# A hybrid encoder block on one core: where the rows of the stream's blocks begin, and how query and key columns are cut

## The chip, the core and the metric

The kernel runs on one core of one Trainium2 chip. The time is device time in microseconds (us) of one execution, and of several runs the median is given. The profile is one execution taken by the hardware profiler. Engines are named as the profile does: PE is TensorE's matmul side, PEld its weight loads, DVE is VectorE, ACT is ScalarE, POOL is GpSimd, SP is SyncE, whose queue issues most transfers.

## The reference

One layer of a streaming encoder over 1040 positions (16 meta tokens and 1024 frames) of width 1024, float32:

```
h = concatenate([meta, x])
h = h + token_mixer(rmsnorm(h), w_in, ..., w_out)      # 4 mLSTM heads and 4 retention heads
h = h + channel_mixer(rmsnorm(h), w_up, w_gate, ffn_conv_w, w_down)
return rmsnorm(h)[16:]

channel_mixer(u): a = causal_dwconv(u @ w_up, 3 taps)
                  (silu(a) * (u @ w_gate)) @ w_down    # width 2816
```

The mixer projects to queries, keys, values and gates, runs a short convolution or a rotation on queries and keys, scans both kinds of heads in chunks, normalises each head, gates it and projects back with w_out.

## The kernel before

**Precision.** Each large product is made of three float32r matmuls: an operand x is kept as hi (rounded) and lo (x minus hi), and hi*hi, hi*lo and lo*hi are added in one PSUM bank. `mm3s` issues the three; its lines are L924 (hi weights, hi stream), L925 (hi weights, lo stream) and L926 (lo weights, hi stream). The first operand is stationary (a 128x128 weight tile), the second moves, up to 512 columns at a time.

**Seven products for eight.** The large products are cut into 2x2 quarters and computed with seven products of sums and differences. So the stream is kept not as two halves but as blocks, one for each of the seven operands. In the gated MLP the blocks are numbered 0 to 6, each a hi and a lo tile of four rows (one for each 128 of the contraction), and each row holds XW = 514 columns: two columns of halo that the 3-tap convolution needs, and 512 of the stream. `ublock` and `fblock` make them: blocks 0, 3, 4 and 5 in the u-tiles (PE rows name them uh_g and ul_g), block 1 in two large tiles (x), blocks 2 and 6 in the pool `fp` (xh and xl). Before, the four rows of a block follow each other at a distance of 514 columns, 2056 bytes.

**The stages in time.** Up to some 673 us: normalisation, the projections of one head after another (`qk_steps`, `o_steps`, `v_steps`), and between their matmuls the side work of the heads (scans, convolutions, normalisations). This side work is dealt into the stream of matmuls by a planner: `watch` keeps a modelled time for each engine (a float32r matmul of n columns counts 0.004 + 0.000445 n us, at least 0.107), and `slot` and `tick` compare these loads with limits (`RULES`) to decide how much side work follows each step. The order that they deal is pinned for PE, DVE and ACT. Query and key products go through `qk_steps`, which cuts the 528 columns of a half at FMC; `v7_steps` uses the same cut. Output gates are cut at OC = [(14, 272), (272, 528)].

From 673 to some 855 us: the output projection (`mixw`, an object of the class `Seven`; PSUM tiles pwx and pwy). Its moving operands alternate between the tiles `fraw` (rows wr) and two ring tiles `rring` (rows rr), as `wr` picks them; one of its five steps has its weights split early into four tiles (w4xh, w4xl) that `four` makes.

From some 845 to 1296 us: the gated MLP's up and gate products. The first pair of column blocks runs over `eight` (`first_up`, `first_gate`); the ten others run over `seven`: seven products, each of four rows times three matmuls, for the gate with one chunk of 512 columns (2 to 514 of a row), for up with the two chunks of UC. Weights are loaded, summed and split by `fstep`, which uses a scratch tile s1.

From 1296 us on: the down projection (`down`, class `Seven`; PSUM tiles pdx and pdy), whose moving operands are slots of the u-tiles, and for the second half of its last quarter 22 small tiles r4h and r4l; then the final normalisation and the output.

**Memory.** Pools on the left grow from the low end of each of the 128 partitions, pools with side="right" from the high end downwards: first `mxp`, later `accp` (the ring tiles), `fp2`, `fp4`, `d2` and `d3` (the r4 tiles). The tiles of the ring begin 32 bytes past a multiple of 64, and so do the r4 tiles, w4xh and block tiles xh.

The one line of `seven` that reads a block, j0 and j1 being the chunk's columns:

```
m = mm3s(pt, [tuple(v[:, o*HB + k*P : o*HB + (k+1)*P] for v in (hi, lo)) for k in range(4)],
         [tuple(v[:, k, j0:j1] for v in xs) for k in range(4)], fresh, n in (1, 5, 6))
```

Of the kernel before, what the change touches and what calls it, by code (L numbers as in the profile page):

```python
# [10 lines left out]
F32 = mybir.dt.float32  # L11
F32R = mybir.dt.float32r
# [5 lines left out]
P = 128  # L18
# [3 lines left out]
SEQ = 1024  # L22
T = META + SEQ
# [6 lines left out]
KD = NFB // 2  # L30
HB = 4 * P
XW = SEQ // 2 + 2
EPS = 1e-6
NEG = -1e30
KSCALE = 128.0 ** -0.5
UN = 1024
SB = 528
# [52 lines left out]
def body(ctx, tc, h_in, vecs, cst, mask_in, rot, w_v0, w_vp, w_g, w_out, w_up, w_gate, w_down, out):  # L90
# [18 lines left out]
    G, PE, V, AC = nc.gpsimd, nc.tensor, nc.vector, nc.scalar  # L109
# [97 lines left out]
    upool = Slots(tc, ctx.enter_context(tc.tile_pool(name="upool", bufs=1)), 1)  # L207
    mix = ExitStack()
    st = Slots(tc, mix.enter_context(tc.tile_pool(name="st", bufs=1)), 1)
    wk = Slots(tc, mix.enter_context(tc.tile_pool(name="wk", bufs=2)), 2)  # L210
    mixed = ExitStack()
    mxp = Slots(tc, mixed.enter_context(tc.tile_pool(name="mxp", bufs=1, side="right")), 1)
    accseg = ExitStack()

    def big(tag, nm, dt=F32R):
        return upool.tile([P, 4 * SB], dt, tag=tag, name=nm)

    def blk(x):
        return x.rearrange("p (k j) -> p k j", k=4)
# [52 lines left out]
    xload(0)  # L272
    V.memset(epsc, EPS)
    V.tensor_scalar(vec[:R36, V_N + 1:V_N + 2], vec[:R36, V_BI:V_BI + 1], 1.0 / 15.0, None, ALU.mult)
# [11 lines left out]
    def pp(name, tag):  # L286
        return ps.tile([P, 512], F32, tag=tag, name=name, bufs=PSB[tag])
# [183 lines left out]
    done = Ready()  # L471
# [316 lines left out]
    def fstep(u, s):  # L788
        kind, i = fseq[u]
        nm = f"{kind}{i}_{s}"  # L790
        fetch(u)
        (w11, w12, r0), (w21, w22, r1) = fraws[u]
        if s:
            fetch(u + 1)
        if u < 2:
            return fsplit(nm, [(r0, r1)[s]])
        if s == 0:
            return fsplit(nm, [r0])
        if s == 1:
            s1 = fpool[0].tile([P, HB], F32, tag="s1", name=f"s1_{u}", bufs=1)  # L800
            V.tensor_tensor(s1, w21, w22, ALU.add)
            V.tensor_tensor(w21, w21, w11, ALU.subtract)
            V.tensor_tensor(w11, s1, w11, ALU.subtract)
            return fsplit(nm, [w11, s1])
        if s == 2:
            V.tensor_tensor(w12, w12, w11, ALU.subtract)
            return fsplit(nm, [w21, w12])
        return fsplit(nm, [w22])
# [231 lines left out]
                steps.append(step)  # L1040
        return steps

    FMC = [(0, 264), (264, SB)]
    OC = [(KEEP, 272), (272, SB)]
    QUAD = {0: (0, 0), 1: (0, 0), 2: (1, 0), 5: (1, 0), 3: (1, 1), 4: (1, 1), 6: (0, 1)}

# [288 lines left out]
    QT = HALF // 2  # L1335
# [159 lines left out]
    wslots = {}  # L1495
# [14 lines left out]
    fpool = []  # L1510
# [26 lines left out]
    def four(x, i):  # L1537
        if ("four", x, i) not in wslots:
            tag = f"x{x}{(2, 6)[i]}"
            wslots["four", x, i] = fpool[0].tile([P, 4 * XW], F32R, name="w4" + tag, tag=tag, bufs=1)  # L1540
        return wslots["four", x, i]

    def wbank(nm, b, j):
# [98 lines left out]
    def post_steps(h, p):  # L1642
# [4 lines left out]
        def stats():  # L1647
            num, mv, den = outs.pop(p)
            z = mxp.tile([P, 4], F32, tag="z", name=f"z{h}_{p}", bufs=4)
            if h < H:  # L1650
# [3 lines left out]
                V.tensor_tensor(z[:, :n], z[:, :n], e2, ALU.max)  # L1654
                V.scalar_tensor_tensor(z[:, :n], z[:, :n], EPS, mv[:, 0:n, 1], ALU.mult, ALU.add)
                yield
# [53 lines left out]
    side = []  # L1710
# [122 lines left out]
    s1 = [st.tile([P, 2 * SB], F32, tag=f"A{i + 1}", name=f"s1_{i}").rearrange("p (k j) -> p k j", k=2) for i in range(2)]  # L1833
# [117 lines left out]
    for k in range(KW):  # L1951
        if k % 2 == 0:
            x = upool.tile([P, 2 * T], F32R, tag=("uh0", "ul0", "uh1", "ul1")[k // 2], name=f"wone{k}")
# [31 lines left out]

    TA, TB = KEEP, KEEP + XW - 2
    blocks = {}

    def xb(i):
        return blocks[i]  # L1990
# [15 lines left out]
    def ftile(nm):  # L2006
        return fp.tile([P, XW + 2], F32, tag="f", name=nm, bufs=5)

# [6 lines left out]
    def spare_out(nm):  # L2015
        return fp4.tile([P, XW + 2], F32, tag="xc", name=nm, bufs=2)

# [45 lines left out]
    def scale_tasks(t0, t1, tag):  # L2063
# [4 lines left out]
        def one(kb):  # L2068
            x = RES[kb][:, t0:t1]
            V.tensor_tensor(x, x, Rb[:, t0:t1], ALU.mult)  # L2070
            last["scaled"] = xsingle(kb, t0, TA + XW if t1 == TB else t1, t0 >= TB)
        return [norm] + [lambda kb=kb: one(kb) for kb in range(KB)]
# [14 lines left out]
    fp = fseg.enter_context(tc.tile_pool(name="fp", bufs=2, reuse_waits="tile"))  # L2087
    Rb = fp.tile([P, T], F32, name="Rb", tag="Rb", bufs=1)
# [15 lines left out]
        wload("A2", k)  # L2104

    def ublock(i):
        return tuple(upool.tile([P, 2 * T], F32R, tag=f"u{x}{i}", name=f"u{x}{i}_g")[:, :4 * XW].rearrange("p (k j) -> p k j", k=4) for x in "hl")

    def fblock(b):
        if b == 5:  # L2110
            return tuple(big(f"t{i}", f"x{i}5")[:, :4 * XW].rearrange("p (k j) -> p k j", k=4) for i in range(2))
        return tuple(fp.tile([P, 4, XW], F32R, name=f"x{x}{b}", tag=f"x{x}{b}", bufs=1) for x in "hl")


    BQ, AQ = [(MB, T)], [(MA, MA + QT), (MA + QT, MB)]
    side = []
# [5 lines left out]
    for t, (st, k) in enumerate(mixw.steps):  # L2122
        if st == "2":
            break
        if t < KW - 2:
            continue
        if st == "65" and k == 5:
            x = fp.tile([P, 4 * XW], F32, name="wm", tag="xl6", bufs=1)
            nc.sync.dma_start(x[:, :2 * D].rearrange("p (k j) -> p k j", k=2), w_out[14:16].rearrange("k p j -> p k j"))
        if st == "65" and k >= 2:  # L2130
            after(mixw.tsum(3, k - 2), last["rsplit"][1])
        elif st == "73" and k < 2:
            after(mixw.tsum(3, KW - 2 + k), last["rsplit"][1])
        if t >= KW - 2:
            mixw.prep(t)
            if t < KW:
                mixw.mms(t)
        for u in range(t, min(t + (3 if st == "4" or t == KW - 2 or (st, k) == ("73", KW - 1) else 2), 4 * KW)):
            mixw.prep(u)
            if mixw.steps[u][0] == "73" and u % 2 and u + 7 not in mixw.four:  # L2140
                mixw.pre4(u + 7)
        if t >= KW:
            mixw.mms(t)
        if st == "4" and k == 0:
            for _ in tail_sum(7, [x[:, b * D:(b + 1) * D] for b in range(2)]):
                pass
        if st == "4" and k == 1:
            pe = pp("pe2", "tr")
            for j in range(2):
                PE.transpose(pe[:, j * P:(j + 1) * P], tail[:, j * P:(j + 1) * P], ident)  # L2150
            for i, y in enumerate(RT):
                V.tensor_tensor(y[:, :, T - 2:], y[:, :, T - 2:], pe[:, :2 * P].rearrange("p (j g t) -> p j g t", j=2, g=4)[:, :, i, :2], ALU.add)
        if st == "4" and k:
            some(3)
        if k == KW - 1:
            mixw.give(st)
            if st == "73":
                for b in (2, 6):
                    blocks[b] = fblock(b)
                side += norm_tasks(*BQ[0]) + scale_tasks(*BQ[0], "tr")  # L2160
# [84 lines left out]
    c0 = {}  # L2245
    gbank = {}
    kept = {(kind, m, half): dram.tile([P, n], F32, name=f"kept_{kind}{m}{half}") for kind, n in (("up", XW), ("ga", HB)) for m in range(2) for half in range(2)}
    UC = [(0, QT), (QT, XW)]

    def eight(kind, half, j0, j1, bank, done):  # L2250
        for m in range(2):
            hi, lo = need((kind, 0, m), 2 - m)
            pt = bank(m)[:, :j1 - j0]
            xs = [xb(kb // 4 if half == 0 else (6, 2)[kb // 4]) for kb in range(KB)]
            mm3s(pt, [tuple(y[:, kb * P:(kb + 1) * P] for y in (hi, lo)) for kb in range(KB)],
                 [tuple(y[:, kb % 4, j0:j1] for y in xs[kb]) for kb in range(KB)], True, True)
            done(m, pt)

    def first_up(half, ci, tags):
        def done(m, pt):  # L2260
            if ci == 0:
                c0[m, half] = ftile(f"c0_{m}{half}")
            AC.copy(c0[m, half][:, slice(*UC[ci])], pt)
            if ci:
                nc.sync.dma_start(kept["up", m, half], c0[m, half][:, :XW])
        eight("up", half, *UC[ci], lambda m: pp(f"pup0_{m}{half}{ci}", tags[m]), done)

    def first_gate(half, j0, j1, tags):
        def bank(m):
# [33 lines left out]
        xcomb(k, QT, XW)  # L2303

    def up_part(i):
        chunks = UC
        def done(m, half, c):
            if isinstance(c, list):
                t = ftile(f"c{i}_{m}{half}")
                for x, (j0, j1) in zip(c, chunks):  # L2310
                    AC.copy(t[:, j0:j1], x)
                c = t
            conv(i, m, half, c)
        return seven("up", i, chunks, done)
# [54 lines left out]
    for i in range(1, NPAIR):  # L2369
        u, g = up_part(i), gate_part(i)  # L2370
# [30 lines left out]
    Rb = dp.tile([P, T], F32, name="Rc", bufs=1)  # L2401
# [78 lines left out]
    for p in (1, 2):  # L2480
# [5 lines left out]
        else:  # L2486
            for mb in (1, 4):
                x = RES[mb][:, OP[2][0]:OP[2][1]]
# [7 lines left out]
def _lay(inputs):  # L2496
# [27 lines left out]
    for h in range(H):  # L2524
        m = i[:META]
        cst[:, C_GV + h] = np.exp(lg[h] * (P - 1 - i)) * KSCALE
        cst[:META, C_GV0 + h] = np.exp(lg[h] * (META - 1 - m)) * KSCALE
        cst[:, C_EPS + h] = EPS * np.exp(-2.0 * lg[h] * (i + 1))
        cst[:, C_GP + h] = np.exp(-lg[h] * (i + 1)) * KSCALE
# [68 lines left out]
```

## Time and profile before

| | |
|---|---|
| runs | 1525.46, 1525.55, 1525.79 us; median 1525.55 |
| profiled execution | span of 1523.9 us from its first to its last instruction; no other time is given for it, and the median stands 1.65 us above the span |
| PE | busy 1487.8 us (98%), 9929 matmul records |
| PEld | 1349.9 us (89%) |
| DVE | 1090.4 us (72%) |
| ACT | 756.4 us (50%) |
| POOL | 72.1 us (5%) |
| granted TensorE clock | 0.995 of full on average |

How to read it: the profile gives each instruction's start and duration. A matmul's duration includes the time in which it drains while the next one already streams, so durations of neighbours overlap, and the pace of a stream of matmuls is the distance from one start to the next. Where the view of instructions in time merges neighbours of the same line, a row has x2 or more and its start is that of the first. Some matmul records can be missing from a trace, so counts of a run are taken from the code.

### The profile page before, as it was taken

How to read it: one execution, taken by the hardware profiler on the slowest of the kernel's cores; microseconds unless marked ns; L12 is line 12 of the kernel's file. 1: busy time of each engine (PE TensorE's matmuls, PEld its weight loads, DVE VectorE, ACT ScalarE, POOL GpSimd, SP SyncE). 2: the span in 40 equal slices, each digit the busy share in tenths (PEclk: the TensorE clock that was granted, in tenths of full speed). 3: DMA queues.
4: the chain of work that ended last, by engine and by line, in shares of the span. 5: the costliest groups of instructions: out<-in, count | busy, mean ns of one | idle time of the engine just before them, and what ended most of it. 6: DMA issues, size and time to landing. Idle time of an engine off the chain costs nothing.

```text
span 1523.9 us, 25488 instructions
## 1 busy us (share of the span) xinstructions
PE 1487.8 (98%) x9929; PEld 1349.9 (89%) x9929; DVE 1090.4 (72%) x2087; ACT 756.4 (50%) x1455; POOL 72.1 (5%) x157
## 2 busy tenths in 40 slices
PE   7989999999999999999999999999999999999997
PEld 7988999998999999987888998999999999888887
DVE  6885868677777677756867787766666666778667
ACT  4465655554655455544454565444444444344443
POOL 1000000000000000000000001222220000000000
PEclk9999999999999999999999999999999999999999
DMA  6022245323632446697333247887772224933213
GB/s 232 2 93 56 90 155 192 111 84 111 200 106 98 131 161 199 194 401 258 108 115 125 77 136 222 209 211 201 177 186 77 83 82 157 369 106 108 97 42 111
DMA packets 104586, 223.81 MB, mean 147 GB/s; under 512 B 10520, under 2 KB 33760, under 8 KB 104288
## 3 DMA queue, kind: packets, MB, share of 16 engines
q1 hardware_dynamic: 89824, 191.68, 37.4%
q0 software_dynamic: 8448, 23.07, 7.6%
q10 hardware_dynamic: 6192, 7.41, 1.4%
q8 instruction: 78, 1.28, 0.3%
q14 instruction: 44, 0.36, 0.1%
HBM read 178.05 MB, written 67.15 MB: 161 GB/s over the span
## 4 chain that ended last, share of the span: by engine, by line
PE 89%; DVE 5%; ACT 2%; DMA 2%; issue 1%; SPq 0%; DVEq 0%; ACTq 0%
PE pdx L926 3%; PE pdx L925 3%; PE pdx L924 3%; PE pup_x L925 2%; PE pup_x L924 2%; PE pup_x L926 2%; PE pga_x L924 2%; PE pga_x L925 2%; PE pga_x L926 2%; PE pdy L926 2%; PE pdy L925 2%; PE pdy L924 2%; PE n L1621 2%; PE pwx L926 2%; PE u L1619 2%; PE pwx L924 2%
## 5 line engine op out<-in xcount | busy, mean ns | idle before, releaser
L783 ACT CAST hi_up<-raw_up 128x512 fp32r<-128x512 f32 (+1 forms) x52 | 36.4, 719 | 106.7 <-PE pga_z L925 60.2
L924 PE MATMUL pup_x<-uh_g,hi_up 128*128 128x256 f32 (+1 forms) x240 | 67.6, 284 | 1.2 <-ACT uh_g L1995 1.2
L784 DVE TENSOR_TENSOR lo_up<-raw_up,hi_up 128x512 fp32r<-128x512 f32 (+1 forms) x52 | 41.3, 809 | 38.3 <-ACT hi_up L783 37.5
L784 DVE TENSOR_TENSOR lo_ga<-fraw_ga,hi_ga 128x512 fp32r<-128x512 f32 (+1 forms) x52 | 41.9, 808 | 37.3 <-ACT hi_ga L783 37.1
L925 PE MATMUL pup_x<-ul_g,hi_up 128*128 128x256 f32 (+1 forms) x240 | 67.7, 284 | 0.1
L926 PE MATMUL pup_x<-uh_g,lo_up 128*128 128x256 f32 (+1 forms) x240 | 66.5, 283 | 0.0
L784 DVE TENSOR_TENSOR lo_d<-rd,hi_d 128x1024 fp32r<-128x1024 f32 (+1 forms) x34 | 37.7, 1113 | 32.8 <-ACT hi_d L783 32.7
L783 ACT CAST hi_ga<-fraw_ga 128x512 fp32r<-128x512 f32 (+1 forms) x52 | 36.4, 719 | 45.5 <-PE pup_z L925 24.1
L926 PE MATMUL pdx<-uh_d,lo_d 128*128 128x512 f32 (+1 forms) x156 | 57.9, 375 | 0.0
L925 PE MATMUL pdx<-ul_d,hi_d 128*128 128x512 f32 (+1 forms) x156 | 57.8, 374 | 0.0
L783 ACT CAST hi_d<-rd 128x1024 fp32r<-128x1024 f32 (+1 forms) x34 | 32.3, 959 | 49.3 <-PE pdy L925 32.5
L926 PE MATMUL pdy<-uh_d,lo_d 128*128 128x512 f32 x132 | 51.9, 393 | 0.0
L925 PE MATMUL pdy<-ul_d,hi_d 128*128 128x512 f32 x132 | 51.7, 392 | 0.0
L924 PE MATMUL pdx<-uh_d,hi_d 128*128 128x512 f32 (+1 forms) x156 | 48.5, 372 | 0.0
L924 PE MATMUL pdy<-uh_d,hi_d 128*128 128x512 f32 x132 | 47.9, 389 | 0.0
L924 PEld LDWEIGHTS pup_x<-uh_g,hi_up 128*128 128x128 f32 x240 | 45.7, 191 | 2.3 <-ACT uh_g L1995 1.4
L924 PE MATMUL pga_x<-uh_g,hi_ga 128*128 128x512 f32 x120 | 47.5, 396 | 0.0
L925 PE MATMUL pga_x<-ul_g,hi_ga 128*128 128x512 f32 x120 | 47.5, 396 | 0.0
L926 PE MATMUL pga_x<-uh_g,lo_ga 128*128 128x512 f32 x120 | 47.1, 393 | 0.0
L925 PEld LDWEIGHTS pup_x<-ul_g,hi_up 128*128 128x128 f32 x240 | 45.8, 191 | 1.0 <-DVE ul_g L1996 0.3
L926 PEld LDWEIGHTS pup_x<-uh_g,lo_up 128*128 128x128 f32 x240 | 45.0, 190 | 0.7
L1688 DVE SCALAR_TENSOR_TENSOR mx<-tr,vec,sig 128x386 f32<-128x386 f32 (+2 forms) x42 | 24.0, 571 | 21.1 <-PE tr L1680 16.0
(1687 smaller groups left out, 5732.4 us busy)
## 6 DMA issues: line engine op xcount, KB each, us to landing
raw_up<-w_up_d SPq DMA_DIRECT2D x22, 512.0 KB, 5.6
fraw_ga<-w_gate_d SPq DMA_DIRECT2D x22, 512.0 KB, 4.3
acts<-cv SPq DMA_DIRECT2D x44, 256.0 KB, 4.6
wsd<-w_down_d POOLq DMA_DIRECT2D x44, 256.0 KB, 6.7
rd<-wsd SPq DMA_DIRECT2D x22, 512.0 KB, 3.5
raw_w<-w_out_d SPq DMA_DIRECT2D x20, 512.0 KB, 7.3
wsw<-raw_w SPq DMA_DIRECT2D x32, 256.0 KB, 3.1
raw_m<-w_out_d SPq DMA_DIRECT2D x14, 512.0 KB, 4.0
```

What stands on the lines that cost most here:

```text
L783: AC.copy(hi[:, o:o + n], x)
L784: V.tensor_tensor(lo[:, o:o + n], x, hi[:, o:o + n].bitcast(F32), ALU.subtract)
L924: m.append(PE.matmul(pt, ah, xh_, start=first and k == 0, stop=False, skip_group_check=True))
L925: PE.matmul(pt, ah, xl_, start=False, stop=False, skip_group_check=True)
L926: m.append(PE.matmul(pt, al, xh_, start=False, stop=last and k == n - 1, skip_group_check=True))
L1619: PE.matmul(up[:, :nv], kw[:L], v, start=True, stop=True)
L1621: PE.matmul(pn[:L, :nv], pt[:L, :L], v, start=True, stop=c == 0)
L1688: return V.scalar_tensor_tensor(dst, tr[:, x0 - t0:x1 - t0], vec[:, g:g + 1], sig(b, p)[:, x0 - a0:x1 - a0], ALU.mult, ALU.mult)
```

## The change

- XR = 528 columns is the new width of a row in all fourteen block tiles; XO = 14 columns at the front of each row stay unused, the halo lies in columns 14 and 15, the stream from column 16 on. `ublock` and `fblock` hand out views that begin at column 14, so that the rest of the code counts columns as before. The tiles of `four` and the tile wm, which share slots with block tiles, get the same size.
- A tile `edge` of 32 bytes is put at the right end ahead of the other pools on that side, so that all of them lie 32 bytes lower: the ring tiles, the r4 tiles, the small tiles of the mixer.
- s1, the scratch of `fstep`, loses its own 2048 bytes and uses the slot of the tile Rb.
- FMC is cut at 272 and not at 264: query and key chunks (and those of the seventh head's values) are 272 and 256 columns wide where they were 264 and 264.
- UC becomes two lists: for the ten pairs, and for one half of the first pair, up is cut at 258 and not at 256 (chunks of 258 and 256); for the other half of the first pair the cut stays at 256, where only 256 columns are there yet.

```diff
+XR = SEQ // 2 + 16
+XO = XR - XW
...
+    ctx.enter_context(tc.tile_pool(name="edge", bufs=1, side="right")).tile([P, 8], F32, name="edge")
     mixed = ExitStack()
...
-            s1 = fpool[0].tile([P, HB], F32, tag="s1", name=f"s1_{u}", bufs=1)
+            s1 = fpool[0].tile([P, T], F32, tag="Rb", name=f"s1_{u}", bufs=1)[:, :HB]
...
-    FMC = [(0, 264), (264, SB)]
+    FMC = [(0, 272), (272, SB)]
...
-            wslots["four", x, i] = fpool[0].tile([P, 4 * XW], F32R, name="w4" + tag, tag=tag, bufs=1)
+            wslots["four", x, i] = fpool[0].tile([P, 4 * XR], F32R, name="w4" + tag, tag=tag, bufs=1)
...
     def ublock(i):
-        return tuple(upool.tile([P, 2 * T], F32R, tag=f"u{x}{i}", name=f"u{x}{i}_g")[:, :4 * XW].rearrange("p (k j) -> p k j", k=4) for x in "hl")
+        return tuple(blk(upool.tile([P, 4 * XR], F32R, tag=f"u{x}{i}", name=f"u{x}{i}_g"))[:, :, XO:] for x in "hl")
     def fblock(b):
         if b == 5:
-            return tuple(big(f"t{i}", f"x{i}5")[:, :4 * XW].rearrange("p (k j) -> p k j", k=4) for i in range(2))
-        return tuple(fp.tile([P, 4, XW], F32R, name=f"x{x}{b}", tag=f"x{x}{b}", bufs=1) for x in "hl")
+            return tuple(big(f"t{i}", f"x{i}5")[:, :4 * XR].rearrange("p (k j) -> p k j", k=4)[:, :, XO:] for i in range(2))
+        return tuple(fp.tile([P, 4, XR], F32R, name=f"x{x}{b}", tag=f"x{x}{b}", bufs=1)[:, :, XO:] for x in "hl")
...
-            x = fp.tile([P, 4 * XW], F32, name="wm", tag="xl6", bufs=1)
+            x = fp.tile([P, 4 * XR], F32, name="wm", tag="xl6", bufs=1)
...
-    UC = [(0, QT), (QT, XW)]
+    UC = [(0, QT + 2), (QT + 2, XW)], [(0, QT), (QT, XW)]
...
-            AC.copy(c0[m, half][:, slice(*UC[ci])], pt)
+            AC.copy(c0[m, half][:, slice(*UC[half == 0][ci])], pt)
...
-        eight("up", half, *UC[ci], lambda m: pp(f"pup0_{m}{half}{ci}", tags[m]), done)
+        eight("up", half, *UC[half == 0][ci], lambda m: pp(f"pup0_{m}{half}{ci}", tags[m]), done)
...
     def up_part(i):
-        chunks = UC
+        chunks = UC[0]
```

## The prediction

> **What bounds the kernel now.** I read the page first, then the stretches, then TensorE's own rows in order of time. The page:
>
> ```profile
> span 1523.9 us, 25488 instructions
> PE 1487.8 (98%) x9929; PEld 1349.9 (89%) x9929; DVE 1090.4 (72%) x2087; ACT 756.4 (50%) x1455; POOL 72.1 (5%) x157
> PEclk9999999999999999999999999999999999999999
> PE 89%; DVE 5%; ACT 2%; DMA 2%; issue 1%; SPq 0%; DVEq 0%; ACTq 0%
> ```
>
> TensorE is busy for 98% of the span at the full granted clock, and 89% of the chain that ended last is matmuls. The stretches say where it is not covered (columns: length, then busy time of each engine):
>
> ```profile
> core 0: us, PE busy (x) PEld busy (x) DVE busy (x) ACT busy (x) POOL busy (x), PEclk, DMA share, GB/s
> 60.00:160.00 100.00, 91.93 (x709) 87.27 (x709) 75.12 (x162) 58.04 (x110) 0.53 (x5) 0.98 0.20 63
> 160.00:260.00 100.00, 97.39 (x768) 91.36 (x767) 75.45 (x167) 58.73 (x125) 2.54 (x14) 1.00 0.46 149
> 260.00:460.00 200.00, 199.32 (x1566) 188.40 (x1565) 148.38 (x351) 112.05 (x237) 5.80 (x36) 1.00 0.38 125
> 1120.67:1134.66 13.99, 13.99 (x62) 11.29 (x61) 8.43 (x13) 6.52 (x11) 2.77 (x4) 1.00 0.97 236
> 1142.13:1160.34 18.21, 18.21 (x154) 18.21 (x153) 12.15 (x21) 9.35 (x18) 0.00 (x0) 1.00 0.24 75
> 1329.77:1343.50 13.73, 13.73 (x62) 11.27 (x60) 10.72 (x15) 5.73 (x9) 0.00 (x0) 1.00 0.42 133
> ```
>
> The last three rows are pieces of the gate, up and down products. Each is a whole run: by the code 60 gate matmuls (five products of 12), 152 up matmuls and 60 down matmuls, with no idle time (the counts beside them include matmuls still under way at an edge). A gate matmul of 512 columns thus costs 13.99/60 = 233.2 ns, a down matmul of 512 columns 13.73/60 = 228.8 ns, an up matmul 18.21/152 = 119.8 ns. Same clock, same width, same weight tiles, and yet 4.4 ns apart. What differs is where the moving rows start. Down reads rows at multiples of 64 bytes. The stream's blocks hold four rows of 514 columns, 2056 bytes, so each row starts 8 bytes further past a multiple of 64 than the one above. One gate product, first matmul of each row and of the next product:
>
> ```profile
> 1120.67 0.40 PE L924 MATMUL pga_x<-uh_g,hi_ga 128*128 128x512 f32 x1
> ...
> 1121.38 0.39 PE L924 MATMUL pga_x<-uh_g,hi_ga 128*128 128x512 f32 x1
> ...
> 1122.07 0.39 PE L924 MATMUL pga_x<-uh_g,hi_ga 128*128 128x512 f32 x1
> ...
> 1122.77 0.40 PE L924 MATMUL pga_x<-uh_g,hi_ga 128*128 128x512 f32 x1
> ...
> 1123.46 0.40 PE L924 MATMUL pga_y<-x,hi_ga 128*128 128x512 f32 x1
> ```
>
> Rows that start 8, 16, 24 and 32 bytes past a multiple of 64 take 0.71, 0.69, 0.70 and 0.69 us for three matmuls.
>
> **The change, part by part.** All positions below are added up from the tile sizes in the code. With rows of 528 columns (33 times 64 bytes) every row starts at a multiple of 64; the halo at columns 14 and 15 puts a gate chunk at column 16, byte 64, and the second up chunk at column 272, a multiple of 64; the first up chunk starts at byte 56. The change removes and adds no instruction and moves no DMA. A duration saved on TensorE in the up, gate and down stages is saved from the end, since nothing else fills those stages: DVE is busy 12.15 of 18.21 us and ACT 9.35.
>
> *Gate*: ten pairs of 84, 840 matmuls, now at 233.2. The fast end is the down row, 228.8, a gain of 3.7 us; the slow end comes from the ring's neighbours below, where an aligned run also took 2.80 us for 12, 233.3, no gain. I take 3.5 ns, since 792 down matmuls stand against a few such runs: 2.9 us.
>
> *Second up chunk*, 258 columns before, 256 after, and *first up chunk*, 256 before, 258 after. One up product before (256 columns at 0, 8, 16, 24 bytes, then 258), aligned 256-column rows from the down stage and from the last quarter of the output projection, and a 258-column chunk that already starts at byte 56:
>
> ```profile
> 1145.97 0.28 PE L924 MATMUL pup_x<-uh_g,hi_up 128*128 128x256 f32 x1
> 1146.32 0.28 PE L924 MATMUL pup_x<-uh_g,hi_up 128*128 128x256 f32 x1
> 1146.68 0.28 PE L924 MATMUL pup_x<-uh_g,hi_up 128*128 128x256 f32 x1
> 1147.05 0.28 PE L924 MATMUL pup_x<-uh_g,hi_up 128*128 128x256 f32 x1
> 1147.41 0.28 PE L924 MATMUL pup_x<-uh_g,hi_up 128*128 128x258 f32 x1
> 1148.85 0.28 PE L924 MATMUL pup_z<-uh_g,hi_up 128*128 128x256 f32 x1
> ...
> 1483.55 0.28 PE L924 MATMUL pdx<-uh_d,hi_d 128*128 128x256 f32 x1
> 1483.89 0.28 PE L924 MATMUL pdx<-uh_d,hi_d 128*128 128x256 f32 x1
> ...
> 836.13 0.28 PE L924 MATMUL pwy<-wl,wl 128*128 128x256 f32 x1
> 838.05 0.28 PE L925 MATMUL pwy<-wl,wl 128*128 128x256 f32 x1
> ...
> 244.22 0.28 PE L924 MATMUL po1x<-u11h,hi_o 128*128 128x258 f32 x1
> 245.30 0.28 PE L924 MATMUL po1x<-u11h,hi_o 128*128 128x258 f32 x1
> ```
>
> Three matmuls of 256 columns take 0.35 us in the row at 0 (116.7 ns each) and 0.36, 0.37, 0.36 in the others. Aligned rows elsewhere take 0.34 for three (113.3) or 1.92 for 16 (120.0). So the width 256 has two paces even when aligned, and the ends are 113.3 and 120. I take 117.3, next to the row of the same stage: 119.8 - 117.3 = 2.5 ns, 840 matmuls, 2.1 us (ends 0 and 5.5). The 258 columns take 1.44 us for 12 now (120.0) and 1.08 for nine at byte 56 (120.0): nothing, with 1 ns either way, 0.8 us.
>
> *Ring*: the 32-byte tile at the right end moves the ring buffers from 32 past a multiple of 64 onto one. The middle run below is a ring tile, the ones around it aligned:
>
> ```profile
> 715.92 0.86 PE L924 MATMUL pwx<-wr,hi_w 128*128 128x512 f32 x3
> ...
> 718.72 0.40 PE L924 MATMUL pwx<-rr,hi_w 128*128 128x512 f32 x1
> ...
> 721.52 0.39 PE L924 MATMUL pwy<-wr,hi_w 128*128 128x512 f32 x1
> ...
> 724.27 0.40 PE L924 MATMUL pwy<-rr,hi_w 128*128 128x512 f32 x1
> ```
>
> Twelve matmuls take 2.80 (aligned), 2.80 (ring) and 2.75 us (aligned). 240 ring matmuls of 512 columns gain 0 to 4.2 ns, at most 1.0 us; I take 0.7. The 96 matmuls whose weights lie in the w4 buffers, at 32 before and 0 after, are bounded the same way, 0 to 0.4; I take 0.2. The first pair (48 gate matmuls and half of its up) gives 0 to 0.4; I take 0.2.
>
> *Quarter buffers* r4 of the down stage move the same way. Their matmuls beside those of the aligned half:
>
> ```profile
> L926 PE MATMUL pdx<-r4h,lo_d 128*128 128x256 f32 x24 | 6.8, 284 | 0.0
> L926 PE MATMUL pdx<-uh_d,lo_d 128*128 128x256 f32 x24 | 6.1, 276 | 0.0
> ```
>
> Eight ns on 132 matmuls is 1.1 us at most, 0 at least; I take 0.4, since the slower aligned pace of 256 columns is met there too.
>
> *Query and key chunks*: 672 pairs of chunks, 264 and 264 before, 272 and 256 after.
>
> ```profile
> 219.21 0.29 PE L924 MATMUL pq1x<-u11h,hi_o 128*128 128x264 f32 x1
> 219.95 0.28 PE L924 MATMUL pq1x<-u11h,hi_o 128*128 128x264 f32 x1
> ...
> 221.88 0.29 PE L924 MATMUL pq1x<-u11h,hi_o 128*128 128x264 f32 x1
> 222.61 0.28 PE L924 MATMUL pq1x<-u11h,hi_o 128*128 128x264 f32 x1
> ...
> 26.99 0.67 PE L995 MATMUL pq<-u12h,hi_q 128*128 128x272 f32 x4
> 28.00 0.66 PE L995 MATMUL pq<-u12h,hi_q 128*128 128x272 f32 x4
> ```
>
> Six take 0.74 and 0.73 us: 123.3 and 121.7, together 245.0. Eight of 272 take 1.01: 126.3, and with 256 columns at 117.3 to 120 that makes 243.6 to 246.3. I take 0, ends 0.9 either way.
>
> *s1 in the slot of Rb* costs nothing: Rb's readers and s1's writer are DVE's, which works in order, and a whole first pair lies between. DVE and ACT writes keep their sizes.
>
> The sum: 2.9 + 2.1 + 0 + 0.7 + 0.2 + 0.2 + 0.4 + 0 = 6.5 us. The span would be 1517.4. The runs' median stands 1.65 us above the profiled span (1525.55 against 1523.9), so I forecast 1519.1 us. All slow ends together give a loss of 1.7 us, all fast ends a gain of 13.7.
>
> **A rule against it.** The Trainium skill, "SBUF — State Buffer", note on SBUF "cachelines", states lines of 16 bytes, with a price for each access that crosses to a new one. By that rule a row at 16 or 32 bytes is as good as one at 0. The trace speaks against it in the up product: 0.37 us at 16 bytes, 0.35 at 0. For it, the gate rows at 16 and 32 are the shortest of the four, 0.69.
>
> **The rivals.**
> *Only 16 bytes count.* Then the gate comes down to its rows at 16 and 32: 4 x 0.69 = 2.76 for 2.79 us, 0.03 in each of 70 products, 2.1 us; up rows at 0 and 16 average 0.36, as now; ring, w4 and quarter, at 32, gain nothing. 2.1 us in all: 1523.5.
> *The slow pace.* Aligned rows lock at 233.3 and 120 as in the runs above: what stays is 0.7 + 0.2 + 0.2 + 0.4 = 1.5 us, 1524.1. Against it: the down stage holds 228.8 over 60 matmuls on end.
> *The fast pace.* Up runs at 113.3 and gate at 228.8: 6.5 + 3.4 + 0.8 = 10.7 us, 1514.9. For it: after the change no row of a run has another start than its neighbours, as in the down stage, where that pace is met.
> *The planner deals again (slower).* Up to 673 us side work is dealt by a modelled load, and a first chunk that is 12 x 0.0036 = 0.04 us longer in that model can flip a choice in each query stage. Between 260 and 460 us TensorE stands idle 0.7 of 200 us, between 160 and 260 us 2.6 of 100. If the 413 us from 260 to 673 fell to the second rate, it would lose some 10 us: 1529. It decides from a loss of 9.6 us on; below that it only eats the gain.
> *Alignment is not the cause*, but the stage: no change, 1525.5. Against it: rows of one product differ, 0.35 and 0.37.
>
> **How the numbers follow.** The forecast has 0.55, with a range of its own of 1516.5 to 1521.5; the fast pace 0.20, the slow pace 0.08, 16 bytes 0.07, the planner 0.06, another cause 0.04. About 0.2%, 3.05 us, is what a measurement of this kernel can tell from no change. Faster: nearly all of the first two and a little of the rest, 0.77. Same: slow pace, 16 bytes, another cause and a part of the planner, 0.18. Slower: 0.05. From 1514.0 to 1523.8 all but some 0.2 is held: the fast pace with every other fast end lies below, part of the slow pace, the planner and another cause above.
>
> **What would show it.** Right: a gate run of 60 in 13.75 to 13.80 us, an up run of 152 in some 18.0, ring runs at 2.75 for 12, the first 673 us of the same length within 2 us. Wrong: gate rows at 0.70 with every row aligned, up rows of 256 at 0.36, or TensorE idle in the query stages after 260 us.

## The result, and the profile after

The changed kernel takes 1528.87 us (median of 13 runs, 1526.58 to 1531.63) against 1525.79 us for the kernel before (13 runs beside them): ratio 1.0017, 95% interval 1.0010 to 1.0024. It is slower by some 3 us, where 1519.1 us was forecast. The profiled execution has a span of 1526.5 us against 1523.9. The page of the changed kernel, its span, busy times and the shares of the chain of waits:

```profile
span 1526.5 us, 25493 instructions
PE 1488.3 (97%) x9929; PEld 1349.9 (88%) x9929; DVE 1089.4 (71%) x2087; ACT 756.8 (50%) x1455; POOL 72.3 (5%) x157
PEclk9999999999999999999999999999999999999999
PE 87%; DVE 6%; ACT 3%; DMA 2%; issue 1%; SPq 0%; DVEq 0%; ACTq 0%
```

TensorE's busy time is 1488.3 us against 1487.8, and the span is longer: matmuls did not get shorter in sum, and idle time came in. The view by stretches of the changed kernel (columns as in the prediction; the last three rows are one run of 60 gate, of 152 up and of 60 down matmuls, from first start to the next start):

```profile
60.00:160.00 100.00, 92.22 (x711) 87.55 (x710) 75.11 (x162) 58.13 (x110) 0.54 (x5) 0.98 0.19 63
160.00:260.00 100.00, 97.13 (x766) 91.06 (x765) 75.22 (x165) 58.58 (x125) 2.58 (x14) 1.00 0.46 149
260.00:460.00 200.00, 197.59 (x1552) 185.30 (x1552) 146.56 (x348) 110.89 (x233) 5.63 (x34) 1.00 0.40 129
...
1123.85:1137.74 13.89, 13.89 (x62) 11.27 (x61) 8.43 (x13) 6.52 (x11) 2.53 (x4) 1.00 0.82 196
1145.24:1163.37 18.13, 18.13 (x154) 18.13 (x153) 12.11 (x21) 9.35 (x18) 0.00 (x0) 1.00 0.24 75
...
1345.41:1359.14 13.73, 13.73 (x61) 11.27 (x60) 8.86 (x14) 4.61 (x8) 0.00 (x0) 1.00 0.38 115
```

The gate run went from 13.99 to 13.89 us, not to 13.75; the up run from 18.21 to 18.13, not to 18.0. From 260 to 460 us TensorE is idle for 2.41 us where it was idle for 0.68.

Two starts give the balance by stage, the output projection's first matmul and the down product's, in time order, first of the kernel before, then of the changed one (whose line numbers are three higher):

```profile
673.39 0.40 PE L924 MATMUL pwx<-wone,hi_w 128*128 128x512 f32 x1
...
1296.08 0.40 PE L924 MATMUL pdx<-uh_d,hi_d 128*128 128x512 f32 x1
```

```profile
676.57 0.40 PE L927 MATMUL pwx<-wone,hi_w 128*128 128x512 f32 x1
...
1298.63 0.63 PE L927 MATMUL pdx<-uh_d,hi_d 128*128 128x512 f32 x2
```

In these two executions 3.18 us are lost before the output projection, 0.63 us are won back up to the down product, and after it the distance stays (2.55 us there, 2.6 at the end). So there are two questions: where the 3.2 us come from, and why rows that all start at multiples of 64 bytes won so little. The gate and ring rows after, in time order (first matmul of each row of one gate product and of the next product; then a ring tile, and an aligned tile behind it, twelve matmuls each):

```profile
1123.85 0.39 PE L927 MATMUL pga_x<-uh_g,hi_ga 128*128 128x512 f32 x1
...
1124.54 0.39 PE L927 MATMUL pga_x<-uh_g,hi_ga 128*128 128x512 f32 x1
...
1125.23 0.39 PE L927 MATMUL pga_x<-uh_g,hi_ga 128*128 128x512 f32 x1
...
1125.92 0.40 PE L927 MATMUL pga_x<-uh_g,hi_ga 128*128 128x512 f32 x1
...
1126.62 0.40 PE L927 MATMUL pga_y<-x,hi_ga 128*128 128x512 f32 x1
```

```profile
721.90 0.40 PE L927 MATMUL pwx<-rr,hi_w 128*128 128x512 f32 x1
...
724.71 0.39 PE L927 MATMUL pwy<-wr,hi_w 128*128 128x512 f32 x1
...
727.46 0.39 PE L927 MATMUL pwy<-rr,hi_w 128*128 128x512 f32 x1
```

Every row is aligned to 64 bytes now. The gate row still takes 0.69 to 0.70 us for three matmuls; of two aligned tiles the ring takes 2.81 us for twelve, wr 2.75. Alignment to 64 bytes is not what sets these paces.

### The profile page after: what moved, and what is told of

Read it like the earlier page. It is cut to its first block, busy times and chain, and to the rows that moved or that the text cites. A ratio compares the mean times of both kernels' runs of the same rounds, so it can differ in the third digit from the quotient of the medians.

```text
span 1526.5 us, 25493 instructions
## 1 busy us (share of the span) xinstructions
PE 1488.3 (97%) x9929; PEld 1349.9 (88%) x9929; DVE 1089.4 (71%) x2087; ACT 756.8 (50%) x1455; POOL 72.3 (5%) x157
## 4 chain that ended last, share of the span: by engine, by line
PE 87%; DVE 6%; ACT 3%; DMA 2%; issue 1%; SPq 0%; DVEq 0%; ACTq 0%
PE pdx L927 3%; PE pdx L928 3%; PE pdx L929 3%; PE pup_x L928 2%; PE pup_x L927 2%; PE pup_x L929 2%; PE pga_x L928 2%; PE pga_x L929 2%; PE pga_x L927 2%; PE pdy L928 2%; PE pdy L927 2%; PE pdy L929 2%; PE n L1624 2%; PE pwx L929 2%; PE u L1622 2%; PE pwx L927 2%
## 5 line engine op out<-in xcount | busy, mean ns | idle before, releaser
L927 PE MATMUL pup_x<-uh_g,hi_up 128*128 128x258 f32 (+1 forms) x240 | 67.3, 283 | 1.8 <-ACT uh_g L1998 1.8
L928 PE MATMUL pup_x<-ul_g,hi_up 128*128 128x258 f32 (+1 forms) x240 | 67.9, 285 | 0.0
L929 PE MATMUL pup_x<-uh_g,lo_up 128*128 128x258 f32 (+1 forms) x240 | 66.4, 283 | 0.0
```

Source lines behind the costliest of these rows:

```text
L927: m.append(PE.matmul(pt, ah, xh_, start=first and k == 0, stop=False, skip_group_check=True))
L928: PE.matmul(pt, ah, xl_, start=False, stop=False, skip_group_check=True)
L929: m.append(PE.matmul(pt, al, xh_, start=False, stop=last and k == n - 1, skip_group_check=True))
```

## The experiments: where the 3 us went

**What stands idle.** The waits of TensorE between 395 and 470 us in the changed kernel (the kernel before has none in that stretch), and the two largest in time order:

```profile
engine line waited for: us in total, times, longest us
PE po3y L927 <- ACT hi_o L478: 0.7, 1, 0.7
PE po3y L929 <- DVE lo_o L483: 0.5, 1, 0.5
PE pm L606 <- PE s L1582: 0.2, 1, 0.2
PE tr L1683 <- DVE mx L1691: 0.2, 1, 0.2
```

```profile
414.04 0.28 PE L929 MATMUL po3x<-uS2h,lo_o 128*128 128x256 f32 x1
415.00 0.39 PE L927 MATMUL po3y<-uS1h,hi_o 128*128 128x258 f32 x1 [0.68 <-ACT hi_o L478]
415.22 0.28 PE L928 MATMUL po3y<-uS1l,hi_o 128*128 128x258 f32 x1
415.98 0.39 PE L929 MATMUL po3y<-uS1h,lo_o 128*128 128x258 f32 x1 [0.48 <-DVE lo_o L483]
```

An output-gate product (po3y) asks for its split weights before ACT and DVE have made them. The order of TensorE's work in the two kernels is the same up to the query products pq2, differs by one place there, and from pq3 to pq5 side work stands in many other places. That fits the planner; three kernels tell it from the rest of the change.

**Chunks of 264 and 264 again, the rest of the change kept.**

```diff
-    FMC = [(0, 272), (272, SB)]
+    FMC = [(0, 264), (264, SB)]
```

> The changed kernel with query and key chunks of 264 and 264 again. Planner theory (the new chunks made the planner deal other work into the query stages from the third on, and that lost 3.1 us; the FFN rows gained 0.7): 1525.3, ratio to the kernel before 0.9997, and the order of TensorE's work up to 673 us that of before. Rival (the loss comes from the moved buffers): ratio 1.0017 to 1.002, as with the whole change.

Measured: 1524.83 us, ratio 0.9995 (0.9986 to 1.0005). TensorE's order up to the output projection is that of before, and the loss is gone.

**Chunks of 272 and 256, but the planner counts each as 264.**

```diff
         n = math.prod(x[1] for x in o.ap[1:])
+        if even[0] and n in (256, 272):
+            n = 264
```

(`even` is set while the matmuls and the evacuation of such a chunk are issued.)

> The changed kernel, chunks 272 and 256 as in it, but the planner's model counts each of these chunks as 264 columns, so that it deals the work as before. Planner theory: the 3.1 us are gone, ratio 0.9997, within 0.0004. Rival (a pair of 272 and 256 is itself slower on TensorE than two of 264, 672 pairs): the loss stays, ratio 1.0017. Between them, by the pair's own durations (243.6 to 246.3 against 245.0 ns): -0.9 to +0.9 us of 1525.

Measured: 1524.71 us, ratio 0.9994 (0.9985 to 1.0002). The same chunks, and up to the output projection exactly the old order: no loss. So the widths themselves cost nothing that can be told; the model's reaction to them did.

**The kernel before with nothing but the new chunks.**

> The kernel before with nothing but the query and key chunks at 272 and 256. Planner theory: slower by about 3.1 us, ratio 1.002, TensorE idle between 395 and 450 us as in the changed kernel. Rival (moved buffers): ratio 1.000.

Measured: 1527.59 us, ratio 1.0016 (1.0007 to 1.0025). Up to the output projection its order is, matmul for matmul, that of the changed kernel. The stretch from 395 to 460 us in the kernel before, in this one and in the one whose planner counts 264:

```profile
395.00:460.00 65.00, 65.00 (x507) 62.04 (x507) 52.24 (x121) 39.46 (x84) 1.55 (x9) 1.00 0.44 137
```

```profile
395.00:460.00 65.00, 63.25 (x493) 58.90 (x493) 51.90 (x122) 37.60 (x80) 1.51 (x9) 1.00 0.48 159
```

```profile
395.00:460.00 65.00, 65.00 (x509) 62.04 (x507) 52.27 (x121) 39.50 (x84) 1.56 (x9) 1.00 0.43 137
```

TensorE is idle for 1.75 us with the new order and not at all with the old one. That is not the whole 3.2 us: TensorE's modelled ends run into the gaps, and added up from start to start, less the pace of the matmuls, the five gaps of that stretch of the changed kernel come to some 2.6 us. Another 0.4 us is there before it (the first matmul of pq3y at 391.42 against 391.03).

By the ratios the new order costs 3.5 us in the changed kernel (1.0017 against 0.9994) and 2.4 in the kernel before. Not all of a run's time is this idle time: the changed kernel's 13 runs have a mean granted clock of 0.9938, the 11 with the model held 0.9951. Within one kernel's runs, 0.001 less of clock goes with some 0.9 us more (an estimate from the clocks and times of all runs here), so some 1.2 us of the difference go with the clock.

## The experiments: what sets the pace of a matmul

**Streams alone.** A kernel of matmuls only, with moving rows and weight tiles at chosen places. A stream looks like this (h, l: places of the hi and lo rows, rs: bytes from row to row; WH, WL: places of the weights):

```
def gate(h, l, rs, n=512, wh=WH, wl=WL, blocks=2, bs=16896, rep=2):
    ...
                x, y = h + bs * b + rs * k, l + bs * b + rs * k
                s += [mm(x, wh + o, n, r), mm(y, wh + o, n, r), mm(x, wl + o, n, r)]
```

> A kernel of matmuls alone: it computes nothing of the block, and its output is rows of the input. Streams of 48 float32r matmuls whose moving rows and weight tiles lie at chosen positions of one buffer, no other engine at work. Theory 1 (what the forecast held: a start at a multiple of 64 bytes makes the pace): every aligned 512-column stream at 228.9 ns, every unaligned one at 232 to 234, the copy of the new gate layout too. Theory 2 (the change of row makes it): one moving row held through a stream gives 228.9 wherever it lies, eight rows in turn give 231.7 at 2112 bytes from row to row and 228.9 at 2048. Theory 3 (the position in some larger power of two makes it): rows held still split into 228.9 and 233.3 by their place within 512 or 2048 bytes, fast at 64 and 320, slow at 448 and 1984, and rows in turn give a mean of what their places give. Theory 4 (the work of the other engines makes it): all aligned streams at one pace here, the gate copy at 228.9 as well.

The stretches of eleven streams, 24 matmuls each from the twelfth start to the thirty-sixth (counts include matmuls still under way at an edge). In order: a copy of the new gate layout; rows 2304 bytes apart; one row held at 0, 32, 64, 128 and 192 bytes past a multiple of 256, weights at multiples of 512; the row at 64 with the weights 64 further; 256 columns held at 0 and at 192; last, a copy of the down product's rows (64 past a multiple of 256, 2048 apart):

```profile
39.73:45.31 5.58, 5.58 (x25) 4.51 (x24) 0.00 (x0) 0.00 (x0) 0.00 (x0) 1.00 0.00 0
150.79:156.23 5.44, 5.44 (x26) 4.50 (x24) 0.00 (x0) 0.00 (x0) 0.00 (x0) 1.00 0.00 0
216.92:222.36 5.44, 5.44 (x25) 4.50 (x24) 0.00 (x0) 0.00 (x0) 0.00 (x0) 1.00 0.00 0
250.21:255.81 5.60, 5.60 (x26) 4.50 (x25) 0.00 (x0) 0.00 (x0) 0.00 (x0) 1.00 0.00 0
283.59:289.08 5.49, 5.49 (x26) 4.51 (x24) 0.00 (x0) 0.00 (x0) 0.00 (x0) 1.00 0.00 0
294.61:300.19 5.58, 5.58 (x25) 4.52 (x24) 0.00 (x0) 0.00 (x0) 0.00 (x0) 1.00 0.01 3
305.78:311.38 5.60, 5.60 (x26) 4.51 (x25) 0.00 (x0) 0.00 (x0) 0.00 (x0) 1.00 0.00 0
549.36:554.80 5.44, 5.44 (x26) 4.50 (x24) 0.00 (x0) 0.00 (x0) 0.00 (x0) 1.00 0.00 0
648.11:650.99 2.88, 2.88 (x27) 2.88 (x25) 0.00 (x0) 0.00 (x0) 0.00 (x0) 1.00 0.02 6
665.18:667.90 2.72, 2.72 (x26) 2.72 (x25) 0.00 (x0) 0.00 (x0) 0.00 (x0) 1.00 0.03 6
821.08:826.68 5.60, 5.60 (x26) 4.54 (x24) 0.00 (x0) 0.00 (x0) 0.00 (x0) 1.00 0.00 0
```

Divided by 24: gate copy 232.5 ns; 226.7 with rows 2304 apart (nine times 256); held at 0, 32, 64, 128, 192: 226.7, 233.3, 228.8, 232.5, 233.3; 226.7 again at 64 once the weights stand at 64 too; 256 columns 120.0 and 113.3; the copy of the down rows 233.3. With no other engine at work the spread is there, so theory 4 falls. Theory 1 falls with the aligned rows at 192, theory 2 with the held rows, which differ. Theory 3 comes nearest, in a form not written down: the pace of a held row goes with the distance from the weight tile to the moving row, modulo 256 bytes, and 0 is best for 512 columns. Weights 32, 128 and 192 bytes further, with the row at 64, agree too: distances 32, 192 and 128, and 233.3, 233.3 and 232.1 ns. Two things do not fit: rows in turn do not give the mean of what their places give (the four held paces average 230.3), and the copy of the down rows, at distance 64 throughout, took 233.3 in both of its streams, where the held row took 228.8 and the kernel's down run 228.8.

**The same, tested on rows that change.**

> Matmuls alone again, nothing of the block is computed. Theory (from the first such run): the distance from the weight tile's start to the moving row's start, modulo 256 bytes, sets the pace of a stream. It expects, for 512 columns held at distances 0, 64, 128, 192: 226.7, 228.9, 232.2 and 233.3 ns whatever the first matmul's moment; for 256 columns 120.0, 117.8, 118.6 and 113.3; and for rows 2112 bytes apart the same four values once the weight tiles stand 576 bytes apart, so that the distance stays (226.7 at 0), while weight tiles 512 bytes apart give 231.7 at every first offset, and rows 2304 bytes apart give the four values with weight tiles 512 apart. Rival (the change of row costs by itself): rows 2112 apart stay at 231.7 with either spacing of the weights, and rows 2304 apart are no better. Second rival (which of two paces a stream falls into is set by the moment at which it starts): the streams with another matmul ahead scatter between the paces at one distance.

Three gate-like streams, 24 matmuls each: rows 2112 bytes apart with weight tiles 576 apart, so that each row has distance 0 from its own weights; rows 2304 apart at distance 0, and at 64:

```profile
683.78:689.34 5.56, 5.56 (x25) 4.50 (x24) 0.00 (x0) 0.00 (x0) 0.00 (x0) 1.00 0.00 0
705.98:711.42 5.44, 5.44 (x25) 4.50 (x24) 0.00 (x0) 0.00 (x0) 0.00 (x0) 1.00 0.00 0
819.72:825.32 5.60, 5.60 (x25) 4.54 (x24) 0.00 (x0) 0.00 (x0) 0.00 (x0) 1.00 0.00 0
```

231.7, 226.7 and 233.3 ns. Rows 2304 apart at distance 0 run as if one row were held, so there a change of row costs nothing by itself. But weight tiles that follow the rows did not help (231.7, forecast 226.7; 230.6 to 231.7 at all four distances): distance to the own weights is not the whole rule. And 64 gave 233.3 here, as the copy of the down rows had, where a held row gave 228.9, so at that distance two paces exist. With another matmul of 64, 100 or 140 columns ahead, 512 columns kept one pace at each of the four distances (within 0.7 ns), while 256 columns at 192 gave 117.8, 113.3 and 117.8. Only this is safe ground for 512 columns: with all rows and all weight tiles at one place modulo 256, every stream took 226.7. For 256 and 258 columns nothing of the kind came out: layouts like the up product's lay between 117.5 and 120.6.

**In the kernel: ring and quarter buffers to multiples of 256.**

```diff
-    ctx.enter_context(tc.tile_pool(name="edge", bufs=1, side="right")).tile([P, 8], F32, name="edge")
+    ctx.enter_context(tc.tile_pool(name="edge", bufs=1, side="right")).tile([P, 56], F32, name="edge")
```

> The changed kernel with chunks of 264 and 264, and the tile at the right end 224 bytes instead of 32, so that ring and quarter buffers start at multiples of 256 (before: 160, changed kernel: 192 past one). Theory (distance of a held moving row from the weight tile, modulo 256): the 192 ring matmuls of 512 columns whose weights are at a multiple of 256 go from 233.3 to 226.7 ns, 1.3 us; the 48 with weights 64 further stay; 180 of 256 columns go towards 120.0, at most 0.9 us back. 1524.0, ratio to before 0.9989. Rival (alignment to 64 bytes is all): as with chunks of 264 and 264 alone, 0.9995, ring runs at 233.

Measured: 1525.10 us, ratio 0.9992 (0.9983 to 1.0001): not told apart from the 0.9995 of its base. The ring's mean pace fell only from 232.1 to 229.9 ns, some 0.5 us in 240 where 1.3 were expected. Its runs follow the tiles wr, which still stand at distance 64: in the run of 24 ring matmuls from 738.00 us on, the first ten average 231.7 ns, the other fourteen 226.6. So a new pace takes some matmuls to settle.

**In the kernel: 192 bytes ahead of the stream's tiles.**

```diff
+    ctx.enter_context(tc.tile_pool(name="pad", bufs=1)).tile([P, 48], F32, name="pad")
     upool = Slots(tc, ctx.enter_context(tc.tile_pool(name="upool", bufs=1)), 1)
```

> The changed kernel with chunks of 264 and 264, and 192 bytes ahead of the stream's tiles, so that these, the down product's rows and the output projection's unringed rows start at multiples of 256 instead of 64 past one. Theory (distance modulo 256): 792 down matmuls of 512 columns from 228.9 to 226.7 ns and 288 of the output projection likewise, 2.4 us; 276 of 256 columns from 117.8 to 120.0, 0.6 us back; gate and up rows, which stand 2112 bytes apart and so pass through all four distances anyway, as before. 1523.0, ratio 0.9983. Rival (alignment to 64 bytes is all): ratio 0.9995, down triples at 687.

Measured: 1522.50 us, ratio 0.9974 (0.9963 to 0.9985). Faster than both kernels.

**Both moves.**

> Both moves together. Theory: 1.0 and 1.8 us add up, 1522.1, ratio 0.9978. Rival: 0.9995.

Measured: 1523.48 us, ratio 0.9984 (0.9975 to 0.9992): not faster than the pad alone. Yet here, with wr at distance 0 too, a ring run of 24 keeps 226.7 ns from its first matmul on (737.16 to 742.60 us).

**The weights moved, not the rows.** From the base with chunks of 264:

```diff
+    ctx.enter_context(tc.tile_pool(name="wpad", bufs=1)).tile([P, 16], F32, name="wpad")
     wsp = Slots(tc, ctx.enter_context(tc.tile_pool(name="wsp", bufs=3)), 3)
...
+    ctx.enter_context(tc.tile_pool(name="pad", bufs=1)).tile([P, 48], F32, name="pad")
     upool = Slots(tc, ctx.enter_context(tc.tile_pool(name="upool", bufs=1)), 1)
```

> The changed kernel with chunks of 264 and 264; the weight tiles start 64 bytes further, the stream's tiles 256 further, so that no moving row changes its place modulo 256 and every distance to the weights falls by 64. If the distance counts: down matmuls of 512 columns (now 64 against 64) at 226.7 ns as if the rows had been moved, triples of 680; ring matmuls at distance 128 at 232.2; gate as before; 1.8 us from down, 0.7 from the output projection, 1522.5, ratio 0.9980. If the row's own place counts: down triples stay at 687, ring at 233.3, ratio 0.9995.

Measured: 1522.47 us, ratio 0.9976 (0.9967 to 0.9985). One run of 60 down matmuls:

```profile
1338.42:1352.02 13.60, 13.60 (x61) 11.27 (x60) 8.84 (x14) 4.60 (x8) 0.00 (x0) 1.00 0.35 116
```

226.7 ns (13.60/60) where it was 228.8, with every row at the same place modulo 256 as before. The distance counts, not the row's own place.

**Rows 2048 bytes apart.** This kernel leaves out the halo of the rows below the first, so it serves the measurement alone.

```diff
+        _, k, j = i
+        o = self.o + 512 * k - 2
+        return self.t[:, o + j.start:o + j.stop]
```

> The changed kernel with chunks of 264 and 264, and the blocks' rows 2048 bytes apart instead of 2112, column 2 of each at a multiple of 256. It changes the computation: the two halo columns of a row share their place with the last two of the row above. Every instruction keeps its width. Theory (distance modulo 256): all gate rows at distance 0, 888 matmuls from 231.7 to 226.7 ns, 4.4 us; second up chunk at distance 0, 118.5 to 120.0, 1.4 us back; first up chunk at 248, 119.7 to 118.8, 0.8 us: 1521.0, ratio 0.9970. Rival 1 (a change of row costs by itself): gate stays at 231.7, ratio 0.9995 or above. Rival 2 (in the whole kernel other engines' traffic sets the pace): gate between, no fixed pattern.

Measured: 1522.44 us, ratio 0.9975 (0.9963 to 0.9986). One run of 60 gate matmuls:

```profile
1119.73:1133.40 13.67, 13.67 (x63) 11.27 (x61) 8.37 (x13) 6.52 (x11) 2.53 (x4) 1.00 0.95 222
```

227.8 ns on average; 214 of the 280 gate triples take exactly 680 ns, 226.7 a matmul. Most of the others are among the first four of a run, while the pace settles. From the first gate matmul of the ten pairs to the down product it takes 385.6 us against 389.8 with rows 2112 apart, 4.1 us less. The whole kernel keeps only a part of it: its profiled run reaches that matmul 3.9 us later than its base, by longer waits for blocks in the first pair and more time at half pace before; that was not taken apart. The gain in the pairs comes near the 5.0 us that the forecast had priced there for alignment to 64 bytes, and nearly all of it is the gate's (231.9 to 227.9 ns).

**All that small pads can move.** Stream tiles, ring and w4 weights to distance 0, quarter buffers left at 192.

> The changed kernel with chunks of 264 and 264; stream tiles, ring and the w4 weight buffers all at multiples of 256, the quarter buffers at 192 past one. Theory (distance modulo 256), against chunks of 264 alone: 792 down matmuls from 228.9 to 226.7 ns, 1.8 us; 336 of the output projection's 512-column matmuls from 228.9 or so, 0.7; 240 ring matmuls from 233.3 or so, 1.6; 0.2 back in 256 columns; quarter buffers at 192 stay near 116.5. 3.9 us in all, 1520.9, ratio to before 0.9970. Rival (the two moves measured one by one did not add up, 0.9974 and 0.9984 with both: what the ring gains is lost elsewhere): 0.9980 or above.

Measured: 1522.08 us, ratio 0.9977 (0.9967 to 0.9986); the down run of 60:

```profile
1339.48:1353.08 13.60, 13.60 (x61) 11.26 (x60) 8.84 (x14) 4.60 (x8) 0.00 (x0) 1.00 0.37 116
```

It beats both kernels, and cannot be told from the pad ahead of the stream's tiles alone. The mean distances from start to start in the profiled runs, in ns (distances over 1.12 times their median left out):

| | gate 512 | up 256 | up 258 | down 512 | ring 512 |
|---|---|---|---|---|---|
| before | 232.9 | 119.2 | 119.8 | 228.9 | 233.2 |
| changed kernel | 231.9 | 118.6 | 119.9 | 228.9 | 232.3 |
| pad of 192 ahead of the stream | 231.6 | 118.2 | 119.5 | 226.7 | 233.2 |
| rows 2048 apart | 227.9 | 119.4 | 119.6 | 228.9 | 232.2 |
| all that can be moved | 231.7 | 118.2 | 119.6 | 226.7 | 226.9 |

Here the ring did gain its 6 ns. That the gain is not seen in the time goes with something else. All three kernels with the moved ring fell, in their profiled runs, into a stretch of half pace in the first pair, which the others did not. The same place in "all that can be moved" and in "pad of 192" (the row's end names the idle time ahead and what ended it):

```profile
872.42 0.39 PE L929 MATMUL pup<-ul_g,hi_up 128*128 128x258 f32 x1 [1.69 <-DVE ul_g L2003]
872.64 0.28 PE L930 MATMUL pup<-uh_g,lo_up 128*128 128x258 f32 x1
...
873.59 0.42 PE L928 MATMUL pup<-uh_g,hi_up 128*128 128x258 f32 x1
...
876.38 0.42 PE L929 MATMUL pup<-ul_g,hi_up 128*128 128x258 f32 x1
...
877.03 0.28 PE L930 MATMUL pup<-x,lo_up 128*128 128x258 f32 x1
```

```profile
874.76 0.39 PE L929 MATMUL pup<-ul_g,hi_up 128*128 128x258 f32 x1 [1.70 <-DVE ul_g L2003]
874.99 0.28 PE L930 MATMUL pup<-uh_g,lo_up 128*128 128x258 f32 x1
...
875.45 0.29 PE L928 MATMUL pup<-uh_g,hi_up 128*128 128x258 f32 x1
```

The same wait, 1.7 us. In the first kernel the matmuls go at full pace for 0.9 us, then at 215 ns for 258 columns (13 from 873.59 to 876.38) and at full pace again; 17 of them cost some 1.5 us. In the second nothing of the kind. The traces hint at why. Each trace records the granted clock; within the kernel its stretches at half last 3.41 or 6.83 us (873.34 to 876.75 here) and start at whole multiples of 3.41 us from each other. In the first kernel the 3.41 us ahead of the stretch, 869.93 to 873.34, hold the wait whole, and TensorE is busy for 1.72 of them. In the second, steps of 3.41 us from its own half stretch at 709.73 put a border at 873.57, inside the wait (873.06 to 874.76), and no stretch follows. So it seems to matter where the wait falls between the borders, and the moved ring brings it 2.3 us forward here. The rule is not sharp: with the weights moved, 3.41 us with TensorE busy for 1.74 at this wait, and as much with 1.65 from 708.50 us on, are followed by no such stretch. That the moved ring meets one in most runs is not shown, but the clocks fit: a mean of 0.9941 over the 11 runs with the ring moved against 0.9955 without (11 runs), and 0.9929 (11) against 0.9940 (7) with the pad.

## Why the prediction was wrong

- **The step that failed** is the base of the sum: "What differs is where the moving rows start", read as alignment to 64 bytes and priced by the down row. With every row aligned the gate stays at 231.9 ns, and aligned streams alone take 226.7 to 233.3. What the runs showed in its place is the distance from weight tile to row, modulo 256: brought to 0, down goes from 228.9 to 226.7 (by moving the rows or the weights), the ring to 226.9, the gate to 227.9. Why down was faster than the gate at the start is known only in part: its rows keep one distance, 64, at which streams alone took 228.9 or 233.3, while the gate rows, 2112 bytes apart, pass through 0, 64, 128 and 192, and such streams took 231.7. Gate: 2.9 us forecast; 232.9 to 231.9 ns, 0.8 us in 840. Second up chunk: 2.1 us forecast; 119.2 to 118.6 ns between the 256-column chunks, 0.5 us. First up chunk: nothing forecast, 119.8 to 119.9. From the first full gate run (962.03 us before, 965.77 after) to the down product the changed kernel won 1.2 us; 0.5 us had been lost between the first gate matmul and that run, where a wait at the first of the ten pairs grew from 1.2 to 1.8 us. That wait is 1.8 in all eight kernels with rows 2112 apart, 1.2 in the two with the old rows and 1.1 with rows 2048 apart; the forecast has no term for it.
- **Ring**, 0.7 us forecast: 233.2 to 232.3 ns on average, 0.2 us in 240. The ring went 32 bytes down to 192 past a multiple of 256, so it came from 224, not from the 160 named with the run of the ring; held rows take 233.3 at both. At 0 it ran at 226.9.
- **Quarter buffers**, 0.4 us: their 132 matmuls went from 118.5 to 116.3 ns, the aligned half beside them from 116.3 to 118.7. Nothing is left.
- **Query and key chunks**, nothing forecast: right for TensorE's own pace. 126.1 and 117.3 ns make 243.4, two of 264 make 243.6.
- **The planner** had the right place and mechanism among the rivals, at 0.06, priced at 10 us with the verdict turning at 9.6. It cost 3.2 us in the profiled run (2.4 to 3.5 by the ratios). That threshold rested on the other terms: with little over 1 us to win and not 6.5, far less than 9.6 us decided. A range that let a loss of a few us stand beside a failed gain would have reached the result.
- **The signs that were there**: aligned runs at 233.3 and at 228.8, aligned 256 columns at 113.3 and at 120.0, gate rows at 32 faster than at 8. They were read as a scatter around one cause, with the "slow pace" at 0.08. Two paces at the same alignment meant that alignment was not the variable. For the gate and the up product that rival (1524.1) and the one of no change (1525.5) came nearest: both give them nothing, and 0.8 and 0.5 us were measured. With the old order the kernel took 1524.7 to 1524.8 us, between the two.
- **s1 in the slot of Rb**: no wait of TensorE in the pairs leads to it; the one that grew ends on ACT's uh_g, and it is short with rows 2048 apart, where s1 has the same slot.
- **Lines of 16 bytes** (the Trainium skill, "SBUF — State Buffer", note on SBUF "cachelines"): held rows at 0, 32 and 64 bytes all start on such a line and take 226.7, 233.3 and 228.8 ns, so this rule does not order them either.

## What to carry to other kernels

Before a layout is changed for the sake of a pace, measure the pace by itself: a kernel of matmuls alone with rows and weights at chosen places gave in one run what three stages of the trace could not. For float32r matmuls of 512 columns, put all weight tiles and all moving rows at the same place modulo 256 bytes, neighbouring tiles included, and let rows follow each other at a multiple of 256; here the pads for it were worth 0.25% of the time. And where a planner deals work by modelled costs, a change of a modelled size is also a change of the order: hold the model's number fixed to see the two apart.

## What the runs showed of the hardware

- The paces met most come as multiples of 6.67 ns: 226.7 and 233.3 for 512 columns, 113.3 and 120.0 for 256 (34, 35, 17 and 18 of them). Other means, such as 228.9 or 231.7, are patterns that repeat after a few matmuls. Distance 0 is not the only fast place: a row held at 240 took 226.7 too. Why the distance modulo 256 counts stays open. So does which of its two paces a stream takes, of 256 columns at 192 or of 512 columns at 64.
- A pace takes up to some ten matmuls to settle when the distance changes: 231.7 ns over the first ten of a ring run behind wr at another distance, 226.6 over the next fourteen.
- After an idle time of 1.7 us TensorE went at half pace for 3.41 us in some profiled runs and not in others. Such a stretch costs some 1.5 us, as much as the ring had to win. The Trainium skill, "TensorE: Matmul & The Clock Gate", Part 1, tells of a free-running window of some 3.4 us by whose activity the clock is halved; the length agrees, and so do the borders at multiples of 3.41 us. It asks for a whole idle window before the clock falls; here one with TensorE busy for 1.72 of 3.41 us was enough, and the measurement decides.
